# The first MLP product of a two-layer encoder by Strassen's scheme, on one core

## The chip, the cores and the metric

The kernel runs on one core of a Trainium2 chip. A core has five engines that run at the same time and wait for one another by semaphores: TensorE (PE; its weight loads are PEld), VectorE (DVE), ScalarE (ACT), GpSimd (POOL) and SyncE (SP, which here only issues DMAs). The metric is the device time of one execution in microseconds (us).

## The reference, cut to what matters

The model has two layers, each a mixer and an MLP, on 512 tokens of width 1024. The change is in the MLP alone:

```python
D_MODEL = 1024; SEQ = 512; D_FF = 4 * D_MODEL; DEPTH = 2
def _rmsnorm(x, g):
    y = x * lax.rsqrt(jnp.mean(x * x, axis=-1, keepdims=True) + RMS_EPS)
    return y * g
def _mlp(x, norm_g, w1, w2):
    h = _rmsnorm(x, norm_g)
    return jnp.square(jax.nn.relu(h @ w1)) @ w2
...
for layer in range(DEPTH):
    x = x + (_even_mixer if layer == 0 else _odd_mixer)(x, ...)
    x = x + _mlp(x, mlp_norm[layer], w_mlp_in[layer], w_mlp_out[layer])
```

All data are float32.

## The kernel before

The residual `xT` is held transposed: eight tiles of 128 features by 512 tokens. Every float32 product is made from three matmuls: each operand is split into a high part, rounded to the type `float32r` by a ScalarE cast, and a low part, the difference, by VectorE, and the product is high x high + high x low + low x high. The products of the activations with the norm's gain are split once per norm (`norm.xg`, a high and a low tile per feature block); the factor per token (`rb`, from `norm.rows()`) is applied where a result leaves PSUM.

Weights come from HBM in pieces of 512 KB. `load_w` issues the DMA on SyncE's queue into a raw buffer (`wraw`, three of them), and splits it into `whi` (line 158, ScalarE) and `wlo` (line 159, VectorE), two buffers each. The cast and the subtraction stand under `tc.high_priority(60)`: the framework lays the instructions of each engine in an order of its own, by readiness and a priority that follows the order of the source, and these two count as if they stood 60 instructions earlier.

`proj_a` makes 256 output features for all 512 tokens: over the 128-row blocks k of the contraction and two column tiles m, three matmuls with 128 x 128 weights and a moving operand 512 wide (lines 177 to 179), into two PSUM banks (tag `acc`, four banks; `aux` has the other four). With eight blocks that is 48 matmuls and two weight pieces, one for every four blocks. Then the two banks are handed to an evacuation function.

`mlp` runs four quarters q of the 4096 hidden features. In each, four calls of `proj_a` make 1024 hidden features from `w1`; the evacuation `ev` takes, per bank, a maximum with 0 and the factor (line 1030, VectorE), the square (1032, ScalarE), and the split into `hh` (1033, ScalarE) and `hl` (1034, VectorE). Four more calls of `proj_a` multiply the quarter's hidden features by `w2` and add to `xT` (line 1044, VectorE). In the last quarter of the last layer `store` does this with the tokens as output rows instead, through `proj_b` (lines 252 to 254), and writes the output.

In the even mixer, the last of the four attention pairs uses projections 256 wide (lines 201 to 203); these are the kernel's 256-wide float32r products of this kind.

Of the kernel before, what the change touches and what calls it, by code (L numbers as in the profile page):

```python
# [9 lines left out]
F32 = mybir.dt.float32  # L10
F32R = mybir.dt.float32r
AF = mybir.ActivationFunctionType
ALU = mybir.AluOpType
# [3 lines left out]
P = 128  # L17
S = 512
# [14 lines left out]
def hybrid_encoder_kernel(  # L33
# [18 lines left out]
    nc = tc.nc  # L52
    mm = nc.tensor.matmul
    act = nc.scalar.activation
    V = nc.vector
    G = nc.gpsimd

    consts = ctx.enter_context(tc.tile_pool(name="consts", bufs=1))
    resid = ctx.enter_context(tc.tile_pool(name="resid", bufs=1))
    wpool = ctx.enter_context(tc.tile_pool(name="wpool", bufs=2))  # L60
# [4 lines left out]
    def acc():  # L65
        return psum.tile([P, 512], F32, tag="acc", bufs=4, name="acc")

    def aux():
        return psum.tile([P, 512], F32, tag="aux", bufs=4, name="aux")
# [6 lines left out]
    gv = consts.tile([P, N_VEC], F32, name="gv")  # L76
# [15 lines left out]
    V.tensor_scalar(nsink, hb[:, 0:8], -1.0, None, op0=ALU.mult)  # L92
    rstd_c = consts.tile([P, 8], F32, name="rstd_c")

    consts.tile([P, 112], F32, name="filler")


    def after(ins, before):
# [63 lines left out]
    def proj_a(w, r0, nk, c0, xs, evac):  # L162

        ps = [acc(), acc()]
        chunks = {}

        def weights(kb):
            if kb not in chunks:
                rows = slice(r0 + kb * P, r0 + min(kb + 4, nk) * P)
                chunks[kb] = load_w([w[rows, c0 : c0 + 256]], 4)  # L170
            return chunks[kb]

        for k, m in [(k, m) for k in range(nk) for m in range(2)]:
            hi, lo = weights(k - k % 4)
            xh, xl = xs[k]
            cs = slice(m * P, (m + 1) * P)
            mm(ps[m], hi[:, k % 4, cs], xh, start=k == 0, stop=False)  # L177
            mm(ps[m], hi[:, k % 4, cs], xl, start=False, stop=False)  # L178
            mm(ps[m], lo[:, k % 4, cs], xh, start=False, stop=k == nk - 1)  # L179
        for m in range(2):  # L180
            evac(m, ps[m])
# [102 lines left out]
    xT = [resid.tile([P, S], F32, tag=f"xT{d}", name=f"xT{d}") for d in range(KT)]  # L284

    def new_xg():
        return [
            (
                resid.tile([P, S], F32R, tag=f"xh{d}", name=f"xh{d}"),
                resid.tile([P, S], F32R, tag=f"xl{d}", name=f"xl{d}"),  # L290
            )
            for d in range(KT)
        ]

    def split_gain(dst, src, gain):
        h, l = dst
        return (
            act(h, src, AF.Copy, scale=gain),
            V.scalar_tensor_tensor(l, src, gain, h.bitcast(F32), op0=ALU.mult, op1=ALU.subtract),  # L299
        )  # L300

    class Norm:


        def __init__(self, vec):
            self.vec = vec
            self.xg = new_xg()
            self.sum = stat.tile([P, S], F32, tag="sqsum", name="sqsum")
            self.n = 0

        def add(self, d):
            split_gain(self.xg[d], xT[d], gv[:, self.vec + d : self.vec + d + 1])
            if self.n == 0:
                act(self.sum, xT[d], AF.Square)
            else:
                sq = stat.tile([P, S], F32, tag="sq", bufs=2, name="sq")
                act(sq, xT[d], AF.Square)
                (G if self.vec == V_MLP else V).tensor_tensor(self.sum, self.sum, sq, op=ALU.add)
            self.n += 1
# [652 lines left out]
    def store(w, hid, pool):  # L972

        rows = {}

        def turn(kb):
            t = kb // 2
            for half in range(2):
                pt = aux()
                for j in range(4):  # L980
                    nc.tensor.transpose(
                        pt[:, j * P : (j + 1) * P],
                        xT[4 * half + j][:, t * P : (t + 1) * P],
                        ident,
                    )
                r = resid.tile([P, S], F32, tag=f"xh{2 * t + half}", name="rows")
                nc.scalar.copy(r, pt)
                rows[t, half] = r

        for half in range(2):  # L990

            def ev(t, ps):
                o = pool.tile([P, S], F32, tag="o", bufs=3, name="o")
                n = 256 if (t, half) == (NB - 1, 1) else 512
                for c in range(0, 512, n):
                    V.tensor_tensor(
                        o[:, c : c + n], ps[:, c : c + n], rows[t, half][:, c : c + n], op=ALU.add
                    )
                    (nc.scalar if c else nc.sync).dma_start(
                        out[t * P : (t + 1) * P, half * 512 + c : half * 512 + c + n],  # L1000
                        o[:, c : c + n],
                    )

            proj_b(
                [w[:, half * 512 : (half + 1) * 512]],
                512,
                hid,
                ev,
                post=None if half else turn,
            )  # L1010

    def mlp(layer, norm, on_final, last=False):
        with tc.tile_pool(name=f"mlp{layer}", bufs=1) as pool:
            rb = None
            for q in range(4):
                hid = [
                    (
                        pool.tile([P, S], F32R, tag=f"hh{k}", name="hh"),
                        pool.tile([P, S], F32R, tag=f"hl{k}", name="hl"),
                    )  # L1020
                    for k in range(8)
                ]
                for c in range(4):

                    def ev(m, ps):
                        nonlocal rb
                        rb = rb or norm.rows()
                        hh, hl = hid[2 * c + m]
                        t = pool.tile([P, S], F32, tag="t", bufs=2, name="t")
                        V.scalar_tensor_tensor(t, ps, 0.0, rb, op0=ALU.max, op1=ALU.mult)  # L1030
                        h = pool.tile([P, S], F32, tag="h", bufs=2, name="h")
                        act(h, t, AF.Square)
                        nc.scalar.copy(hh, h)
                        V.tensor_tensor(hl, h, hh.bitcast(F32), op=ALU.subtract)

                    proj_a(w1[layer], 0, 8, q * 1024 + c * 256, norm.xg, ev)
                if q == 3 and last:
                    store(w2[layer, 3072:4096], hid, pool)
                    continue
                for d0 in range(0, KT, 2):  # L1040

                    def ev2(m, ps):
                        d = d0 + m
                        V.tensor_tensor(xT[d], xT[d], ps, op=ALU.add)  # L1044
                        if q == 3:
                            on_final(d)

                    proj_a(w2[layer], q * 1024, 8, d0 * P, hid, ev2)
# [251 lines left out]

    even_mixer(n_mlp0)
    mlp(0, n_mlp0(), lambda d: n_odd().add(d))
    odd_mixer(n_odd(), n_mlp1)

    mlp(1, n_mlp1(), None, last=True)


# [75 lines left out]
```

## Time and profile before

| | before |
|---|---|
| median of 3 runs | 1361.17 us (1361.14 to 1361.97) |
| the profiled execution | 1362.33 us, of which its span is 1360.4 us |
| TensorE busy | 1340.6 us, 6210 matmuls |
| VectorE busy | 766.6 us |
| ScalarE busy | 591.2 us |
| GpSimd busy | 67.9 us |
| DMA | 124.64 MB, mean 92 GB/s |

A row of a group gives source line, engine, operation, tiles written <- read, shape, count, then busy us and mean ns of one, then the engine's idle us just before and what ended it. A row of a timeline gives start, duration, engine, line, and what was run, with the idle time before it in brackets. Neighbouring instructions of an engine overlap in their durations, so how long one takes its place in a stream is read from the starts.

### The profile page before, as it was taken

What the parts mean: (1) busy time and instruction counts of PE and PEld (TensorE: products, weight loads), DVE (VectorE), ACT (ScalarE), POOL (GpSimd) and SP (SyncE); (2) the same over time, 40 slices, a digit from 0 to 9 for tenths busy, and PEclk for the clock granted to TensorE, in tenths of its full rate; (3) what the DMA queues carried; (4) which work ended last, traced back from release to release, by engine and by line L of the source; (5) the groups of instructions that cost most, each with busy time, mean ns of one, the idle gap of its engine ahead of it and who ended that gap; (6) DMA issues with size and microseconds to landing.
All of it is one profiled execution on the core that took longest, in us unless ns stands there. A gap on an engine that the chain in (4) does not pass through costs nothing.

```text
span 1360.4 us, 16216 instructions
## 1 busy us (share of the span) xinstructions
PE 1340.6 (99%) x6210; PEld 1117.6 (82%) x6210; DVE 766.6 (56%) x1227; ACT 591.2 (43%) x1008; POOL 67.9 (5%) x80
## 2 busy tenths in 40 slices
PE   7999999999999999999999999999999999999998
PEld 6889887788888888888888888888888888888887
DVE  6788887633434434565758448547575344343433
ACT  4788775422313323344645445435354233142331
POOL 0223333000000000000000000000000000000000
PEclk9999999999999999999999999999999999999999
DMA  5322312333233223331221331321233333322322
GB/s 162 95 77 85 100 63 85 94 106 95 93 95 106 93 93 97 105 107 62 78 93 47 93 108 47 93 93 47 95 100 99 93 94 101 100 93 93 99 90 91
DMA packets 129502, 124.64 MB, mean 92 GB/s; under 512 B 9472, under 2 KB 122128, under 8 KB 129424
## 3 DMA queue, kind: packets, MB, share of 16 engines
q1 hardware_dynamic: 123648, 120.21, 28.4%
q10 hardware_dynamic: 5744, 3.37, 0.9%
q8 instruction: 49, 0.80, 0.2%
q14 instruction: 29, 0.24, 0.1%
q0 software_dynamic: 32, 0.01, 0.1%
HBM read 120.43 MB, written 3.15 MB: 91 GB/s over the span
## 4 chain that ended last, share of the span: by engine, by line
PE 90%; DVE 5%; ACT 2%; DMA 1%; issue 1%; SPq 0%; ACTq 0%; POOL 0%; DVEq 0%
PE acc L177 22%; PE acc L179 22%; PE acc L178 22%; PE acc L252 4%; PE acc L253 4%; PE acc L254 4%; PE aux L1204 1%; PE aux L1205 1%; PE aux L1206 1%; PE acc L201 1%; PE acc L203 1%; PE acc L202 1%; DVE wlo L159 1%; DMA qk<-in_x_dram 1%; PE aux L1191 1%
## 5 line engine op out<-in xcount | busy, mean ns | idle before, releaser
L158 ACT CAST whi<-wraw 128x1024 fp32r<-128x1024 f32 (+2 forms) x227 | 230.2, 1014 | 638.7 <-PE acc L178 530.5
L159 DVE TENSOR_TENSOR wlo<-wraw,whi 128x1024 fp32r<-128x1024 f32 (+2 forms) x218 | 261.0, 1197 | 290.6 <-ACT whi L158 289.4
L177 PE MATMUL acc<-xh,whi 128*128 128x512 f32 x784 | 305.2, 389 | 1.4 <-DVE xT L849 1.4
L178 PE MATMUL acc<-xl,whi 128*128 128x512 f32 x784 | 305.3, 389 | 0.3 <-DVE xl L299 0.3
L179 PE MATMUL acc<-xh,wlo 128*128 128x512 f32 x784 | 305.1, 389 | 0.0
L177 PE MATMUL acc<-hh,whi 128*128 128x512 f32 x448 | 174.3, 389 | 0.0
L178 PE MATMUL acc<-hl,whi 128*128 128x512 f32 x448 | 174.3, 389 | 0.0
L179 PE MATMUL acc<-hh,wlo 128*128 128x512 f32 x448 | 174.3, 389 | 0.0
L177 PEld LDWEIGHTS acc<-xh,whi 128*128 128x128 f32 x784 | 147.2, 188 | 32.5 <-DVE xT L849 1.8
L178 PEld LDWEIGHTS acc<-xl,whi 128*128 128x128 f32 x784 | 147.2, 188 | 31.3 <-DVE xl L299 1.0
L179 PEld LDWEIGHTS acc<-xh,wlo 128*128 128x128 f32 x784 | 147.2, 188 | 30.8 <-DVE wlo L159 0.2
L178 PEld LDWEIGHTS acc<-hl,whi 128*128 128x128 f32 x448 | 84.1, 188 | 17.5
L177 PEld LDWEIGHTS acc<-hh,whi 128*128 128x128 f32 x448 | 84.1, 188 | 17.4
L179 PEld LDWEIGHTS acc<-hh,wlo 128*128 128x128 f32 x448 | 84.1, 188 | 17.4
L1030 DVE SCALAR_TENSOR_TENSOR t<-acc,rstd_b 128x512 f32<-128x512 f32 x64 | 43.7, 691 | 77.1 <-PE acc L179 77.0
L1044 DVE TENSOR_TENSOR xT<-xT,acc 128x512 f32<-128x512 f32 x56 | 38.3, 687 | 74.8 <-PE acc L179 74.8
L252 PE MATMUL acc<-whi,xh 128*128 128x512 f32 x160 | 63.5, 397 | 0.0
L253 PE MATMUL acc<-wlo,xh 128*128 128x512 f32 x160 | 63.0, 394 | 0.0
L254 PE MATMUL acc<-whi,xl 128*128 128x512 f32 x160 | 62.8, 394 | 0.0
L201 PE MATMUL acc<-whi,xh 128*128 128x384 f32 (+1 forms) x160 | 52.6, 331 | 0.0
L202 PE MATMUL acc<-wlo,xh 128*128 128x384 f32 (+1 forms) x160 | 52.6, 329 | 0.0
L203 PE MATMUL acc<-whi,xl 128*128 128x384 f32 (+1 forms) x160 | 52.1, 326 | 0.0
(230 smaller groups left out, 1911.2 us busy)
## 6 DMA issues: line engine op xcount, KB each, us to landing
wraw<-in_w_mlp_in_dram SPq DMA_DIRECT2D x64, 512.0 KB
wraw<-in_w_mlp_out_dram SPq DMA_DIRECT2D x64, 512.0 KB
wraw<-in_w_in_o_dram SPq DMA_DIRECT2D x48, 512.0 KB
wraw<-in_w_out_o_dram SPq DMA_DIRECT2D x16, 512.0 KB
wraw<-in_w_in_e_dram SPq DMA_DIRECT2D x48, 128.0 KB
wraw<-in_w_in_e_dram SPq DMA_DIRECT2D x12, 256.0 KB
wraw<-in_w_out_e_dram SPq DMA_DIRECT2D x4, 512.0 KB
wraw<-in_w_out_e_dram SPq DMA_DIRECT2D x8, 256.0 KB
```

Of the source, the lines that this page charges most:

```text
L158: nc.scalar.copy(hu, used)
L159: eng.tensor_tensor(lu, used, hu.bitcast(F32), op=ALU.subtract)
L177: mm(ps[m], hi[:, k % 4, cs], xh, start=k == 0, stop=False)
L178: mm(ps[m], hi[:, k % 4, cs], xl, start=False, stop=False)
L179: mm(ps[m], lo[:, k % 4, cs], xh, start=False, stop=k == nk - 1)
L201: mm(o, lh, hi[:, k, :ncols], start=kb + k == 0, stop=False)
L202: mm(o, lh, lo[:, k, :ncols], start=False, stop=False)
L203: mm(o, ll, hi[:, k, :ncols], start=False, stop=kb + k == KT - 1)
L252: mm(o, lh, hi[:, k, :ncols], start=kb + k == 0, stop=False)
L253: mm(o, lh, lo[:, k, :ncols], start=False, stop=False)
L254: mm(o, ll, hi[:, k, :ncols], start=False, stop=kb + k == KT - 1)
L1030: V.scalar_tensor_tensor(t, ps, 0.0, rb, op0=ALU.max, op1=ALU.mult)
```

## The change

A unit is now 512 hidden features: two blocks of 256. Units 0 and 1 (the first quarter) keep `proj_a`. Units 2 to 7 of each layer are computed by seven products in place of eight, by Strassen's scheme in Winograd's form. The 1024 rows of the contraction are paired (even and odd 128-blocks), the 512 columns of the weights are halved, and so are the 512 tokens.

- `combine(i)`, called after each `proj_a` of units 0 and 1, makes once per layer the four sums of activations for one pair of feature blocks (two scaled ScalarE copies, four VectorE operations 256 wide, a cast and a subtraction 1024 wide).
- `load` brings the weights of a unit: A11, A12 and A22 by plain DMAs from SyncE into `sraw` (three buffers), the sums S1 and S3 by a plain DMA of A21 and a second DMA with accumulation, issued from GpSimd, into `ssum` (five buffers). S1 and S3 are asked for two units ahead, A11, A12 and A22 one.
- `total` makes S2 = S1 + A11 and S4 = S2 + A12 on VectorE. `high` and `low` split a block's four 128 x 256 weight tiles, for product j during product j - 2; products 0 and 1 of a unit are split in the unit before.
- `product` is 2 column tiles x 4 pairs x 3 matmuls with a moving operand 256 wide, into the two halves of one PSUM bank.
- `run` is the order of a unit: the seven products, four copies of a bank to SBUF (`keep`), three sums, four results. A result is evacuated 2 x 256 at a time. The last result of a unit is carried into the next one, or finished at once when the second product follows (`more` false).
- `run` stands in `tc.manual_schedule` for ScalarE and VectorE: within the region each of the two issues its instructions in the order of the source. The order on the other engines, and where instructions from outside the region fall among these, stay with the framework.
- `store` takes its output tiles from the tag `s` (five buffers) in place of `o` (three). A filler in the pool of constants is smaller.

The diff, cut to its core:

```diff
-    consts.tile([P, 112], F32, name="filler")
+    consts.tile([P, 80], F32, name="filler")
...
-                o = pool.tile([P, S], F32, tag="o", bufs=3, name="o")
+                o = pool.tile([P, S], F32, tag="s", bufs=5, name="o")
...
+        BLOCKS = ("A11", "A12", "S2", "S1", "S3", "S4", "A22")
+        INPUTS = ("B11", "B21", "U2", "U1", "T3", "B22", "T4")
...
+        def combine(self, i):
+            for m in range(2):
+                act(t, xT[d], AF.Copy, scale=gv[:, norm.vec + d : norm.vec + d + 1])
...
+            V.tensor_tensor(c[:, 0], b11, b12, op=ALU.subtract)
+            V.scalar_tensor_tensor(c[:, 1], c[:, 0], -1.0, b22, op0=ALU.mult, op1=ALU.subtract)
+            V.tensor_tensor(c[:, 2], b22, b12, op=ALU.subtract)
+            V.scalar_tensor_tensor(c[:, 3], c[:, 1], -1.0, b21, op0=ALU.mult, op1=ALU.subtract)
+            nc.scalar.copy(h, c)
+            V.tensor_tensor(l, c, h[:].bitcast(F32), op=ALU.subtract)
...
+                if name[0] == "S":
+                    nc.sync.dma_start(r[name], self.source(u, "A21"))
+                    second = self.source(u, "A22" if name == "S1" else "A11")
+                    G.dma_start(r[name], second, accum_op=ALU.add)
+                else:
+                    nc.sync.dma_start(r[name], self.source(u, name))
...
+        def product(self, u, j, ps, start):
+            for m in range(2):
+                o = ps[:, m * 256 : (m + 1) * 256]
+                for i in range(4):
+                    mm(o, h[:, i, cs], bh, start=first, stop=False, skip_group_check=True)
+                    mm(o, h[:, i, cs], bl, start=False, stop=False, skip_group_check=True)
+                    mm(o, l[:, i, cs], bh, start=False, stop=i == 3, skip_group_check=True)
...
+            a, b, c = acc(), aux(), acc()
+            self.product(u, 0, a, True)
+            load(u + 1, "A11")
+            ahead(2, False)          # high of product 2
+            lows()                   # low halves of results that are due
+            for step in last:        # the carried-over result (1, 0)
+                step()
+            ahead(2, True)           # low of product 2
+            self.product(u, 1, b, True)
+            s1 = keep(a); ahead(3, False); lows(); self.total(u, "S4"); ahead(3, True)
+            self.product(u, 2, a, False)
+            load(u + 1, "A12"); ahead(4, False); t = add(s1, b); result(0, 0, t, 1); ahead(4, True)
+            self.product(u, 3, c, True)
+            s2 = keep(a); ahead(5, False); lows(); ahead(5, True)
+            self.product(u, 4, a, False)
+            s5 = keep(c); load(u + 2, "S1"); load(u + 2, "S3"); ahead(6, False); ahead(6, True)
+            self.product(u, 5, c, False)
+            s3 = keep(a); load(u + 1, "A22"); ahead(7, False); t = add(s5, s3)
+            result(1, 1, t, -1); ahead(7, True); self.total(u + 1, "S2")
+            self.product(u, 6, a, False)
+            ahead(8, False); lows(); t = add(s2, c); result(0, 1, t, 1); ahead(8, True)
+            last.append(lambda: result(1, 0, a, -1))
+            if not more:
+                lows(); last.pop()(); lows()
...
-                    proj_a(w1[layer], 0, 8, q * 1024 + c * 256, norm.xg, ev)
+                for c in range(2):
+                    u = 2 * q + c
+                    if u < 2:
+                            proj_a(w1[layer], 0, 8, u * 512 + c2 * 256, norm.xg, ev)
+                            seven.combine(2 * u + c2)
...
+                    with tc.manual_schedule(
+                        engines={mybir.EngineType.DVE, mybir.EngineType.Activation}
+                    ):
+                        seven.run(u, evac, c == 0)
```

In the diff as shown, statements of `run` that stand on lines of their own are joined, and the comments are added.

More of the change, by code (lines that the diff above doesn't have):

```diff
@@ L1014, in mlp, with tmp, ev, evac @@
             rb = None
+            seven = Seven(pool, w1[layer], norm)
+            def tmp():
+                return pool.tile([P, S], F32, tag="s", bufs=5, name="s")
             for q in range(4):
[L1016 to L1021, printed above, removed]
-                ]
[L1023 to L1034, printed above, removed]
-                    proj_a(w1[layer], 0, 8, q * 1024 + c * 256, norm.xg, ev)
+                blocks = [
+                    [
+                        pool.tile([P, 2, S], F32R, tag=f"h{x}{k}", name=f"h{x}")
+                        for x in ("h", "l")
+                    ]
+                    for k in range(4)
+                ]
+                hid = [(h[:, m], l[:, m]) for h, l in blocks for m in range(2)]
+                for c in range(2):
+                    u = 2 * q + c
+                    if u < 2:
+                        for c2 in range(2):
+                            def ev(m, ps):
+                                nonlocal rb
+                                rb = rb or norm.rows()
+                                h, l = blocks[2 * c + c2]
+                                t = tmp()
+                                V.scalar_tensor_tensor(
+                                    t, ps, 0.0, rb, op0=ALU.max, op1=ALU.mult
+                                )
+                                act(t, t, AF.Square)
+                                nc.scalar.copy(h[:, m], t)
+                                V.tensor_tensor(
+                                    l[:, m], t, h[:, m].bitcast(F32), op=ALU.subtract
+                                )
+                            proj_a(w1[layer], 0, 8, u * 512 + c2 * 256, norm.xg, ev)
+                            seven.combine(2 * u + c2)
+                            if (u, c2) == (0, 1):
+                                seven.load(2, ("A11", "A12"))
+                            if (u, c2) == (1, 0):
+                                seven.load(2, ("S1", "S3"))
+                                for j in range(2):
+                                    seven.high(2, j)
+                                    seven.low(2, j)
+                        if u == 1:
+                            seven.load(2, ("A22",))
+                            seven.total(2, "S2")
+                            seven.load(3, ("S1", "S3"))
+                        continue
+                    def evac(fb, half, ps, sign, c=c):
+                        hs = slice(half * 256, (half + 1) * 256)
+                        h, l = (x[:, :, hs] for x in blocks[2 * c + fb])
+                        t = ps if sign > 0 or half else tmp()
+                        two = lambda v: v[:].rearrange("p (m t) -> p m t", m=2)
+                        V.scalar_tensor_tensor(
+                            two(t),
+                            two(ps),
+                            0.0,
+                            rb[:, hs].unsqueeze(1).to_broadcast([P, 2, 256]),
+                            op0=ALU.max if sign > 0 else ALU.min,
+                            op1=ALU.mult,
+                        )
+                        def high():
+                            act(t, t, AF.Square)
+                            nc.scalar.copy(h, two(t))
+                        def low():
+                            V.tensor_tensor(l, two(t), h.bitcast(F32), op=ALU.subtract)
+                        return high, low
+                    with tc.manual_schedule(
+                        engines={mybir.EngineType.DVE, mybir.EngineType.Activation}
+                    ):
+                        seven.run(u, evac, c == 0)
```

122 lines of the change are left out of this document (added).

## The prediction

> **What bounds the kernel now.** I read the page from the top: busy time, then the 40 slices of 34 us (each digit a tenth), and then the timelines.
>
> ```profile
> span 1360.4 us, 16216 instructions
> PE 1340.6 (99%) x6210; PEld 1117.6 (82%) x6210; DVE 766.6 (56%) x1227; ACT 591.2 (43%) x1008; POOL 67.9 (5%) x80
> ...
> PE   7999999999999999999999999999999999999998
> PEld 6889887788888888888888888888888888888887
> DVE  6788887633434434565758448547575344343433
> ACT  4788775422313323344645445435354233142331
> POOL 0223333000000000000000000000000000000000
> PEclk9999999999999999999999999999999999999999
> ```
>
> TensorE is busy in all but the first slice, at full granted clock; POOL is idle from slice 8 on. The MLPs (about 246 to 594 us and 1015 us to the end) have VectorE and ScalarE under half busy. So time here falls only with the time of the matmul stream, as long as nothing else becomes late. How long a matmul takes its place in the stream is read from starts, not durations: first the 256-wide ones that the even mixer has (36 rows in a row; first, last, and a weight load), then VectorE in one second-product stretch.
>
> ```profile
> 155.79 0.28 PE L202 MATMUL acc<-wlo,xh 128*128 128x256 f32 x1
> 159.98 0.28 PE L201 MATMUL acc<-whi,xh 128*128 128x256 f32 x1
> 159.98 0.19 PEld L202 LDWEIGHTS acc<-wlo,xh 128*128 128x128 f32 x1
> ...
> 354.86 1.37 DVE L1030 SCALAR_TENSOR_TENSOR t<-acc,rstd_b 128x512 f32<-128x512 f32 x2 [2.68 <-PE acc L179]
> 356.40 1.23 DVE L159 TENSOR_TENSOR wlo<-wraw,whi 128x1024 fp32r<-128x1024 f32 x1 [0.17 <-ACT whi L158]
> 357.96 1.29 DVE L1034 TENSOR_TENSOR hl<-h,hh 128x512 fp32r<-128x512 f32 x2 [0.33 <-ACT hh L1033]
> 361.84 1.22 DVE L159 TENSOR_TENSOR wlo<-wraw,whi 128x1024 fp32r<-128x1024 f32 x1 [2.59 <-ACT whi L158]
> 365.74 1.37 DVE L1030 SCALAR_TENSOR_TENSOR t<-acc,rstd_b 128x512 f32<-128x512 f32 x2 [2.68 <-PE acc L179]
> ```
>
> 256 wide: 4.19 us over 35 intervals, 0.1197 us each, every one with its own weight load. 512 wide: L1030 follows the end of each call of 48 matmuls, 354.86 to 365.74, 0.2267 us each. Two 256-wide ones cost 6% more than one 512-wide: that is the price of halving.
>
> **The matmuls.** A unit of 512 columns has 2x8x2x3 = 96 matmuls of 512: 21.76 us. By the scheme it has 7 products x 2 column tiles x 4 x 3 = 168 of 256: 20.11 us. Gain 1.65 us in each of 12 units (6 per layer): **-19.8 us**. Each product takes 24 x 0.1197 = 2.87 us.
>
> One page of the Trainium skill bears on this price: "TensorE: Matmul & The Clock Gate", section "Back-to-back issue gap", gives N/2.4 + 2.5 ns, so 109 ns at 256 and 216 at 512, by which the gain would be an estimated 2.4 us per unit, 29 in all. The starts above do not agree (119.7 and 226.7), and the measured ones decide.
>
> **ScalarE and VectorE inside a unit.** Prices by form:
>
> ```profile
> L159 DVE TENSOR_TENSOR wlo<-wraw,whi 128x1024 fp32r<-128x1024 f32 x197 | 242.1, 1229 | 287.5 <-ACT whi L158 287.2
> L158 ACT CAST whi<-wraw 128x1024 fp32r<-128x1024 f32 x199 | 209.5, 1053 | 629.5 <-PE acc L178 528.4 <-PE acc L254 64.6 <-issue 34.6
> L1030 DVE SCALAR_TENSOR_TENSOR t<-acc,rstd_b 128x512 f32<-128x512 f32 x64 | 43.7, 691 | 77.1 <-PE acc L179 77.0
> L1034 DVE TENSOR_TENSOR hl<-h,hh 128x512 fp32r<-128x512 f32 x64 | 41.4, 689 | 10.7 <-ACT hh L1033 10.7
> L1032 ACT ACTIVATE h<-t 128x512 f32<-128x512 f32 x64 | 36.6, 619 | 0.0
> L1033 ACT CAST hh<-h 128x512 fp32r<-128x512 f32 x64 | 36.0, 610 | 0.0
> L1208 ACT COPY of<-aux 128x512 f32<-128x512 f32 x16 | 9.1, 584 | 10.5 <-PE aux L1206 10.3
> L622 DVE TENSOR_TENSOR mixa_f<-aux,mixa_f 64x256 f32<-64x256 f32 x16 | 6.7, 418 | 0.3
> L298 ACT ACTIVATE xh<-xT,gv 128x512 fp32r<-128x512 f32 x24 | 17.1, 714 | 6.4 <-DVE xT L849 6.4
> ```
>
> Before, a unit has four weight splits and four evacuations: VectorE 4x1.23 + 4x(0.69+0.69) = 10.4 us, ScalarE 4x1.05 + 4x(0.62+0.61) = 9.1. After: VectorE 7 `low` and 2 `total` of 1.23, 4 evacuations and 4 low halves of 0.69, 3 sums of 0.69: 18.7 us of 20.1, 93%. ScalarE 7 `high` 1.05, 4 `keep` 0.58, 4 squares and casts 1.23: 14.6 us. So VectorE is nearly a second bound, and in source order. By product (0 to 6), VectorE has 2.6, 3.2, 2.6, 1.9, 1.2, 3.8, 3.3 us against 2.87. I laid the lists against each other with a handover of 0.04 us (`whi` to `wlo` in the rows above), neighbours overlapping by 0.06 (two of 0.69 take 1.29 to 1.37). Backlog starts in product 5 and reaches 2.0 us at the next unit's start. The first unit of a pair (c = 0) starts with empty lists and waits for nothing. In the second, ScalarE's `keep` of product 0 stands behind the cast of the carried-over result, and ends 0.34 us before product 2 may write that bank; the one before product 4 has 0.31 us, the weights of product 3 0.66. The lower end is therefore 0; with a handover of 0.15 and no overlap 1.75 us per second unit, 10.5 in all. I take 0.4, nearest to the measured handover, x 6 pairs: **+2.4** (0 to 10.5).
>
> **Where a pair ends.** The second product (`proj_a` on `w2`) needs its weight splits W0 at once and W1 after 24 matmuls, 5.4 us, hidden rows 4, 5 then, rows 6, 7 at 8.2 us. Its ScalarE and VectorE steps stand outside the ordered region and have the earlier priority (60), so W0 can go in during products 5 and 6; the covering work is these two products. After product 6 VectorE still has the rest of its backlog (2.0), W1, two low halves, one evacuation and the 1.2 us of ScalarE between them: rows 6, 7 are done 6.8 us after it if W1 goes into ScalarE's gap, 9.4 to 10.9 if W1 goes ahead of everything. Stall 0 to 2.6; I take 0.5, nearer the first because the gap is there, x 6: **+3** (0 to 16). Without that cover, see the first rival. `w2`'s own raw loads have three buffers that nothing else uses in these units.
>
> **The first two units of each layer** keep the old matmuls and get four `combine`: ScalarE 2x0.71 + 1.05, VectorE 4x0.42 + 1.23, so 10 and 12 us, and the first splits and sum of unit 2 (3.7).
>
> ```profile
> core 0: us, PE busy (x) PEld busy (x) DVE busy (x) ACT busy (x) POOL busy (x), PEclk, DMA share, GB/s
> 246.00:289.00 43.00, 42.81 (x189) 35.48 (x190) 23.62 (x30) 17.02 (x26) 0.00 (x0) 1.00 0.33 104
> ...
> 376.50:420.00 43.50, 43.50 (x194) 36.03 (x193) 15.27 (x16) 8.43 (x8) 0.00 (x0) 1.00 0.31 97
> ```
>
> VectorE comes to 39 of 43 us. The weight splits go first and have 5.4 us for 2.3 of work, so one foreign 1.23 us step ahead of them is covered; two are not quite. I take 1 per layer: **+2** (0 to 10). What is left over spills into the second product, where VectorE has 28 us free (second row).
>
> **DMAs.** A unit loads 7 pieces of 512 KB for 4. One piece now:
>
> ```profile
> 352.21 0.37 SPq L137 DMA_DIRECT2D wraw<-in_w_mlp_out_dram  x1
> ...
> 353.20:355.30 2.10, 2.10 (x11) 1.75 (x10) 0.44 (x1) 0.00 (x0) 0.00 (x0) 1.00 0.85 250
> ...
> hb<-in_heads_dram POOLq DMA_DIRECT2D x1, 12.0 KB, 6.7
> ```
>
> (The issue on SyncE's timeline; a row of the busy times by window, the DMA engines' share and GB/s last; the one issue from POOL, KB and us to landing.) It lands 3.1 us after issue and takes 1.8 us of the 16 engines; seven take 12.5 of 20.1 us, accumulation counted twice 16. SP issues five (1.9 us) in place of four. Plain pieces are asked for four products (11.5 us) or more ahead; they wait on SP for buffers read one or two products earlier, and what stands behind them (the next pieces, `w2`'s) has that lead too. The two accumulating ones go through POOL, wait there for their first piece, and have only each other behind them. The tight one is `S1`: asked for in product 4, needed in product 5 of the next unit, 8 products or 23 us, when both units belong to one pair (4 places; else a second product of 43.5 us lies between). No accumulating transfer is in the trace: as cheap as a plain one 3.1; dear, by the one POOL transfer (6.7 us for 128 rows) scaled to 512 rows, 26.8, so 29.9 with the first piece, 6.9 late. I take cheap, as a 512 KB piece is the nearest in kind: **0** (0 to +28). Five output buffers in place of three, and the smaller filler: 0 (the tail's wait for out DMAs is 1.4 us at most).
>
> **Sum.** -19.8 + 2.4 + 3 + 2 = -12.4 on the span of 1360.4, so 1348.0. That execution took 1362.33 in all; the three runs have 1361.17 at the median, 0.77 over the span: I predict 1348.8.
>
> **Rivals.**
> *The second product's first split comes late.* If W0 stands behind the ordered lists, ScalarE reaches it only after the last hidden cast, and the first matmul waits some 5.4 us (rest of the lists 3.1, split 2.3) at each of 6 pair ends: 32 in place of 3, 1378, slower. It decides once a pair end costs 2.6 us. For: ScalarE and VectorE are both fuller there. Against: the priority, and `whi` is free after product 4. 0.10.
> *VectorE overflows.* Operations 10 to 15% dearer than the rows give 1.1 to 1.7 us per second unit, 2.5 per pair end, 3 at the start: 8 + 15 + 3 - 19.8 = +6 at worst, about -1 midway: 1360, no change. For: 93% full, slack of 0.3 us. Against: the forms have the same prices everywhere in the trace. 0.15.
> *Accumulation is late:* 28 more, 1377. For: nothing shows its price. Against: the lead is seven times a plain piece. 0.06.
> *Loads do not overlap matmuls.* A load lasts 0.19 us; if each 256-wide matmul took that, a unit would take 31.9, 10 more than now: 1361 + 122 = 1483. Against: 35 intervals of 0.1197. 0.01. [...]
>
> **Chances.** The forecast's case 0.68, its own range 1341 (no stalls) to 1358. A run tells about 0.2% (2.7 us) from no change. Faster: 0.68 and a third of the overflow, 0.73; same: half of the overflow and a little of the late cases, 0.10; slower: late split, late sums, the rest of the overflow, 0.17. Range 1340 to 1368: the overflow whole, half-late splits.
>
> **What would show it.** Right: 7074 matmuls and loads (864 more); 256-wide starts 0.12 us apart; units 20.1 us from one first product 0 to the next; DVE near 890 us, ACT near 680; 143 MB moved. Wrong: idle TensorE before product 2 or 4 released by a ScalarE copy (lists), before the first `w2` matmul of a quarter released by `wlo` or `hl` (pair end), VectorE waiting for a DMA of `ssum` (accumulation), or 256-wide starts above 0.125 us.

## The result and the profile after

| | before | after |
|---|---|---|
| median of 4 runs each, same chip | 1361.16 us (1361.05 to 1361.97) | 1344.36 us (1343.98 to 1344.74) |
| the profiled execution | 1362.33 us, span 1360.4 us | 1344.74 us, span 1343.0 us |

The ratio is 0.9875 (95% interval 0.9858 to 0.9892): 16.8 us faster, where 12.4 were forecast. The page of the changed kernel, its busy times and the slices that answer to those of before:

```profile
span 1343.0 us, 18186 instructions
PE 1322.5 (98%) x7074; PEld 1142.8 (85%) x7074; DVE 874.8 (65%) x1363; ACT 676.3 (50%) x1116; POOL 99.6 (7%) x104
...
PE   8999999999999999999999999999999999999998
...
DVE  6788887864837647586748448547588567484553
ACT  4788776542624426444745445435366245262451
POOL 0222432110100000000000000000000000010000
PEclk9999999999999999999999999999999999999999
...
DMA packets 148519, 143.63 MB, mean 107 GB/s; under 512 B 10049, under 2 KB 141137, under 8 KB 148433
```

864 more matmuls take 18.1 us less busy time, and TensorE is as full as before from the second slice on. VectorE rose by 108 us and ScalarE by 85 without becoming the bound. Where the time went is read by stages, cut at the first matmul of each: a row gives the stretch, its length, then busy us and instructions of each engine, the granted clock, the DMA share and GB/s. The changed kernel's last three calls of the first quarter's first product (the first call runs ahead of the norm's factor), the second product behind them, a pair of units, the second product after it, and the last second product of the layer:

```profile
246.85:279.51 32.66, 32.66 (x145) 27.03 (x144) 26.00 (x39) 19.76 (x29) 2.44 (x2) 1.00 0.47 146
279.51:323.03 43.52, 43.52 (x193) 36.04 (x192) 21.49 (x26) 12.79 (x15) 2.74 (x3) 1.00 0.71 172
323.03:363.35 40.32, 40.32 (x338) 40.31 (x337) 29.98 (x34) 25.17 (x34) 5.13 (x4) 1.00 0.66 150
363.35:407.11 43.76, 43.76 (x195) 35.96 (x193) 20.62 (x24) 10.96 (x13) 0.00 (x0) 1.00 0.43 127
531.47:575.02 43.55, 43.55 (x194) 36.05 (x193) 24.55 (x31) 17.79 (x25) 0.00 (x0) 1.00 0.30 97
```

Of the kernel before, the same three calls, and the two stages that answer to a pair and the second product after it:

```profile
246.52:279.18 32.66, 32.66 (x145) 27.04 (x144) 18.85 (x24) 12.80 (x20) 0.00 (x0) 1.00 0.36 113
...
322.70:366.22 43.52, 43.52 (x193) 36.05 (x192) 19.16 (x23) 14.68 (x21) 0.00 (x0) 1.00 0.32 97
366.22:409.74 43.52, 43.52 (x193) 36.05 (x192) 16.57 (x19) 10.51 (x13) 0.00 (x0) 1.00 0.31 97
```

All six pairs take 40.31 or 40.32 us in place of 43.52: 3.20 x 6 = 19.2 us. The three calls of the first quarter take 32.66 in both kernels. The five second products that follow a pair lie between 43.55 and 43.76, 0.9 us in all over 43.52. The rest lies outside the MLPs' pairs: the first of those three calls in layer 0 starts 0.3 later, the odd mixer 0.6 shorter, and the stretch from the start of the last matmul to the end of the span 1.1 longer (4.98 for 3.89). 0.3 - 19.2 + 0.9 - 0.6 + 1.1 = -17.5, against the spans' difference of 17.4.

### The profile page after: what moved, and what is told of

Same layout as the page of the kernel before. It is cut to its first block, busy times and chain, and to the rows that moved or that the text cites. A ratio compares the mean times of both kernels' runs of the same rounds, so it can differ in the third digit from the quotient of the medians.

```text
span 1343.0 us, 18186 instructions
## 1 busy us (share of the span) xinstructions
PE 1322.5 (98%) x7074; PEld 1142.8 (85%) x7074; DVE 874.8 (65%) x1363; ACT 676.3 (50%) x1116; POOL 99.6 (7%) x104
## 2 busy tenths in 40 slices
DMA packets 148519, 143.63 MB, mean 107 GB/s; under 512 B 10049, under 2 KB 141137, under 8 KB 148433
## 4 chain that ended last, share of the span: by engine, by line
PE 90%; DVE 5%; ACT 2%; DMA 1%; issue 1%; POOL 0%; ACTq 0%; SPq 0%; DVEq 0%
PE acc L177 16%; PE acc L178 16%; PE acc L179 16%; PE acc L1116 5%; PE acc L1115 5%; PE acc L1114 5%; PE acc L252 4%; PE acc L253 4%; PE acc L254 4%; PE aux L1458 1%; PE aux L1459 1%; PE aux L1460 1%; PE acc L201 1%; PE acc L203 1%; PE acc L202 1%; PE aux L1116 1%
## 5 line engine op out<-in xcount | busy, mean ns | idle before, releaser
L159 DVE TENSOR_TENSOR wlo<-wraw,whi 128x1024 fp32r<-128x1024 f32 (+2 forms) x170 | 201.2, 1183 | 170.1 <-ACT whi L158 168.8
L177 PE MATMUL acc<-xh,whi 128*128 128x512 f32 x400 | 155.8, 389 | 0.7 <-DVE xT L849 0.7
L178 PE MATMUL acc<-xl,whi 128*128 128x512 f32 x400 | 155.9, 390 | 0.3 <-DVE xl L299 0.3
L179 PE MATMUL acc<-xh,wlo 128*128 128x512 f32 x400 | 155.8, 390 | 0.3 <-DVE wlo L159 0.3
L177 PEld LDWEIGHTS acc<-hh,whi 128*128 128x128 f32 x448 | 84.1, 188 | 17.4
L179 PEld LDWEIGHTS acc<-hh,wlo 128*128 128x128 f32 x448 | 84.1, 188 | 17.4
L177 PEld LDWEIGHTS acc<-xh,whi 128*128 128x128 f32 x400 | 75.1, 188 | 16.9 <-DVE xT L849 1.1
L178 PEld LDWEIGHTS acc<-xl,whi 128*128 128x128 f32 x400 | 75.1, 188 | 16.5 <-DVE xl L299 1.2
L179 PEld LDWEIGHTS acc<-xh,wlo 128*128 128x128 f32 x400 | 75.1, 188 | 16.4 <-DVE wlo L159 0.9
L1114 PE MATMUL acc<-uh,whi 128*128 128x256 f32 x288 | 81.5, 283 | 0.0
L1115 PE MATMUL acc<-ul,whi 128*128 128x256 f32 x288 | 81.5, 283 | 0.0
L1116 PE MATMUL acc<-uh,wlo 128*128 128x256 f32 x288 | 81.5, 283 | 0.0
```

The source lines that it names most:

```text
L159: eng.tensor_tensor(lu, used, hu.bitcast(F32), op=ALU.subtract)
L1114: mm(o, h[:, i, cs], bh, start=first, stop=False, skip_group_check=True)
L1115: mm(o, h[:, i, cs], bl, start=False, stop=False, skip_group_check=True)
L1116: mm(o, l[:, i, cs], bh, start=False, stop=i == 3, skip_group_check=True)
```

## The experiments

The kernel before ran 1361.7 to 1362.0 us (medians) on the same chips as the experiments. Each is an edit of the changed kernel, but for the one that is an edit of the kernel before.

**What the gain is made of: the halves without the scheme.** The kernel before, with the matmuls of units 2 to 7 cut into two of 256:

```diff
-                    proj_a(w1[layer], 0, 8, q * 1024 + c * 256, norm.xg, ev)
+                    proj_a(w1[layer], 0, 8, q * 1024 + c * 256, norm.xg, ev, q > 0)
```

> Edit: the kernel before, with each 512-wide matmul of units 2 to 7 of the first product cut into two of 256 tokens (192 per unit, same weights loaded twice, no seven products). Theory (a 256-wide matmul takes 0.120 us in any such stream, a 512-wide one 0.2267): a pair takes 46.1 in place of 43.5 us, 6 x 2.56 = 15.4 us more: 1376.6; then the omitted eighth product is worth 19.2 + 15.4 = 34.6 us and halving takes 15.4 of it. Rival (256-wide matmuls cost half of a 512-wide one, and the shortfall against 7/8 of the time lies elsewhere): 1361.2 within 1.

Measured 1377.71 us (1376.88 to 1379.44), ratio 1.0119 (1.0105 to 1.0133). Its pair, by window:

```profile
321.73:367.80 46.07, 46.07 (x386) 46.07 (x384) 19.24 (x23) 14.60 (x20) 0.00 (x0) 1.00 0.30 93
```

46.07 us over 384 matmuls is 0.1200 each. Halving alone costs 2.55 us per pair, 15.3 in all (16.0 by the medians), and leaving out the eighth product brings 46.07 - 40.32 = 5.75 per pair, 34.5 in all. The net gain is the small difference of the two: the stream's price of a 256-wide matmul, 6% above half a wide one, takes nearly half of what the scheme saves.

**The order by hand.** `tc.manual_schedule` removed; the framework orders ScalarE and VectorE there too:

```diff
-                    with tc.manual_schedule(
-                        engines={mybir.EngineType.DVE, mybir.EngineType.Activation}
-                    ):
-                        seven.run(u, evac, c == 0)
+                    seven.run(u, evac, c == 0)
```

> Edit: the ordered region around the unit is taken away, so the framework orders ScalarE and VectorE in the units too; the work is the same. Theory (the source order is what leaves every product its operands in time: a bank copy 0.6 us, the weights of product 3 1.0 us ahead in the second unit of a pair): another order puts some copy or split later than these margins, and the six pairs take more than 40.32 us each, 3 to 15 us in all: 1347 to 1359. Rival (the order is worth nothing, there is room for any): 1344.4 within 1 us, pairs 40.3 us.

Measured 1344.83 us (1343.99 to 1345.67), ratio 0.9874 (0.9858 to 0.9891): no difference. The windows of a pair and of the second product after it:

```profile
324.56:364.88 40.32, 40.32 (x338) 40.31 (x337) 31.80 (x37) 25.31 (x34) 5.13 (x4) 1.00 0.79 181
364.88:408.42 43.54, 43.54 (x194) 36.05 (x193) 18.29 (x21) 10.54 (x13) 0.00 (x0) 1.00 0.32 99
```

The pair is as long as before the edit and the second product has even lost its 0.22 us, so the rival held: the written order is worth nothing in time here. The framework's own order finds the slack too.

**The stall at a pair's end.** `low` of product 8 (the next unit's second split, which nothing needs soon) put after the last results (at the end of the branch `not more`) where the second product follows:

```diff
-            ahead(8, True)
+            if more:
+                ahead(8, True)
...
+                ahead(8, True)
```

> Edit: where a pair ends, the low part of the next unit's product 1 is made after the last results in place of before them (same instructions). Theory: the stall of the second product (0.1 to 0.2 us at hidden rows 6 and 7, five times, the last low half landing 8.4 us after product 6 where 8.2 are to be had) is VectorE's queue; 1.14 us less ahead of the results takes it away, the five second products take 43.52 in place of 43.74 us: 1 us less, 1343.4. Rival: the second product's own weight splits set it, and it stays at 43.74: 1344.4.

Measured 1344.16 us (1343.21 to 1345.96), ratio 0.9872 (0.9857 to 0.9886), and the second products stay at 43.72 and 43.74. VectorE's timeline, after the last matmul of the pair:

```profile
365.29 0.68 DVE L1271 SCALAR_TENSOR_TENSOR s<-s,rstd_b 128x512 f32<-128x512 f32 x1
367.32 0.69 DVE L1285 TENSOR_TENSOR hl<-s,hh 128x512 fp32r<-128x512 f32 x1 [1.35 <-ACT hh L1282]
367.93 0.68 DVE L1271 SCALAR_TENSOR_TENSOR s<-acc,rstd_b 128x512 f32<-128x512 f32 x1
369.34 1.23 DVE L159 TENSOR_TENSOR wlo<-wraw,whi 128x1024 fp32r<-128x1024 f32 x1 [0.72 <-ACT whi L158]
370.52 0.69 DVE L1285 TENSOR_TENSOR hl<-s,hh 128x512 fp32r<-128x512 f32 x1
```

The 1.22 us of `low` are gone from the way, but the last result (367.93) must still follow the low half of the result before it, in the order of the source, and VectorE stands idle for 1.35 us in front of that; then `w2`'s next split goes first. The step that was moved was not the one that the chain hung on. In a kernel below that also puts the last result ahead of those low halves (the third of those that do unit 1 by the scheme) the second products are 43.54 or 43.55, as they are in the free order: the stall of 0.2 us is this order's doing.

**How full VectorE is.** Two more subtractions of 128x1024 in every unit, writing the same low part again:

```diff
             ahead(3, True)
+            ahead(3, True)
+            ahead(3, True)
```

> Edit: the low part of product 3's weights is computed three times in place of once in each unit (the same values), 2.3 us more of VectorE's queue, 21 us of work for a unit of 20.16 us. Theory (VectorE in source order is almost a second bound, its lists leave 1.0 us before product 3 in the second unit of a pair and 3 us more in the first): the first unit stays free, the second waits 1.0 to 1.5 us before products 3 and 4: 6 to 9 us in all, 1350.5 to 1353.5. Rival (VectorE at 93% of a unit only looks full, its work lies beside the matmuls with room): under 1 us, 1344.4 to 1345.4.

Measured 1355.76 us (1355.34 to 1355.9), ratio 0.9955 (0.994 to 0.997): 11.4 us lost, where 6 to 9 were expected. A pair's window, and TensorE's waits in that window (us in all, times, longest):

```profile
323.72:366.09 42.37, 40.98 (x337) 40.46 (x336) 34.80 (x38) 24.86 (x34) 5.13 (x4) 1.00 0.64 144
```

```profile
PE acc L1116 <- DVE slo L1104: 1.2, 1, 1.2
PE acc L1114 <- ACT s L1128: 0.2, 1, 0.2
```

Each pair is 2.05 us longer. Where, the starts of the matmuls show; this is the second unit of the pair, at product 3:

```profile
352.78 0.28 PE L1115 MATMUL acc<-ul,shi 128*128 128x256 f32 x1
354.23 0.39 PE L1116 MATMUL acc<-uh,slo 128*128 128x256 f32 x1 [1.17 <-DVE slo L1104]
354.45 0.28 PE L1114 MATMUL acc<-uh,shi 128*128 128x256 f32 x1
```

The three subtractions write one tile, so the first matmul of product 3 that reads the low half (L1116) waits for the last of them. There the changed kernel has 1.25 us of slack (1.0 before the product starts, below, and two matmuls), and 2.5 us were added (3.74 for the three, 1.22 for one): 1.3 are missing. By starts the stream loses 1.33 us at this matmul and 0.10 at the next, 0.49 more before product 4, which waits for a ScalarE copy, and only 0.15 in the whole first unit, whose lists start empty: 2.07 in all. The waits above are shorter, 1.4 together, as a matmul counts there as busy for 0.28 us and takes its place in the stream for 0.12. So it is the slack at one deadline that decides, not VectorE's busy time, which is 34.8 of 42.4 us; the theory held in where the waits come (the second unit, before products 3 and 4), with 1.9 us there in place of 1.0 to 1.5. The waits have the names that the forecast's list stall would have had.

**The accumulating transfers.** First, with the second DMA of each sum left out; S1 and S3 are then A21 alone:

```diff
-                    G.dma_start(r[name], second, accum_op=ALU.add)
```

> Edit: the 24 accumulating transfers from GpSimd are left out, so S1 and S3 are A21 alone (the sums are not formed). Theory: the transfers cost nothing in the units (they land 7.9 us after issue, asked for 23 us ahead) and 1.1 us at the end of the kernel, where SyncE's and GpSimd's closing steps are longer than before: the time from the last matmul's start to the end falls from 4.98 to about 3.9 us, the pairs stay at 40.32, so about 1343.3. Rival A: the longer end has another cause: it stays at 5.0, 1344.4. Rival B: the transfers also slow something in the units or the first quarter: more than 1.5 us gained, seen in the pairs or between them.

Measured 1344.12 us (1343.13 to 1346.03), ratio 0.9871 (0.9857 to 0.9886), pairs 40.32: the transfers cost nothing that this can tell. Whether they lengthen the end stays open. From the start of the last matmul to the end of the span it took 4.98 us in the changed kernel's profiled run and 4.33 without the accumulation, but the other kernels with it had 4.1 to 4.96; without it, the kernel before had 3.89 and its halved form 4.02.

Then the sums asked for one unit later in the source:

```diff
-            load(u + 2, "S1")
-            load(u + 2, "S3")
+            if u > 2:
+                load(u + 1, "S1")
+                load(u + 1, "S3")
```

> Edit: S1 and S3 are asked for in product 4 of the unit before (units 4 to 7), where the kernel asks two units ahead: one product (2.9 us) before S2 needs S1, in place of eight. Theory (an accumulating transfer lands 7.9 us after issue, behind a plain piece of 3.1, so S1 needs 11 us, and VectorE in source order then holds everything behind S2): S2 comes about 6 us late in four units per layer, and a wait of 4 to 6 us follows in each (product 1 of the next unit, or the end of the pair): 32 to 48 us, 1376 to 1392. Rival A (it lands like a plain piece, 6.2 us for both): 1 to 2 us late, about 8 x 1: 1352. Rival B (the lead is worth nothing, there is room behind S2): 1344.4 within 1.

Measured 1344.87 us (1344.38 to 1345.32), ratio 0.9876 (0.9862 to 0.9889): no loss. GpSimd's timeline shows why (issue of the sum S1 of unit 4; VectorE's use of it, S2, starts at 362.23):

```profile
343.65 1.28 POOL L1076 DMA_DIRECT2D ssum<-in_w_mlp_in_dram  x1 [46.89 <-DMA ssum<-in_w_mlp_in_dram]
```

18.6 us of lead in place of 28.7 (issue at 333.61, use at 362.35 in the changed kernel). The later request took 10 us of lead, but the DMA still goes out 11 us before product 4 of unit 3 (354.6 us), behind which it stands in the source. It waits for its plain piece, issued at 337.91 behind a piece of `sraw` that had waited for a buffer; in the changed kernel the plain piece was issued at 328.93, when a split had set its own buffer free. So the position in the source is only part of what sets the lead: the buffers and SyncE's queue are the rest.

To make them late indeed, the sums of units 4 to 7 were asked for in the unit before, and their accumulations held behind a GpSimd operation on one column that reads the `keep` made during product 5:

```diff
+                        with tc.issue_after(gate):
+                            G.dma_start(r[name], second, accum_op=ALU.add)
...
+            if 2 < u < 7:
+                gate = pool.tile([P, 1], F32, tag="gate", bufs=2, name="gate")
+                g = G.tensor_tensor(gate, s3[:, 0:1], s3[:, 0:1], op=ALU.add)
+                self.load(u + 1, ("S1", "S3"), g.ins)
```

> Edit: the accumulating transfers of S1 and S3 of units 4 to 7 are held on GpSimd's queue behind a one-column GpSimd addition that reads the bank copy of product 5 in the unit before, so they start some 0.8 us into that product; S2 is due 4.8 us into it. (In e5_sums_late the transfers still started 18.6 us ahead of S2, since the framework issued them as soon as their buffer was free.) Theory (an accumulating transfer takes 7.9 us to land, and what stands behind S2 in VectorE's order waits with it): S2 about 4 us late; about 3 us lost before product 1 of the next unit inside a pair, 4 us at the end of a pair, 2 + 2 such places per layer: 28 us, 1372. Rival A (it lands like a plain piece, 3.1 us): S2 is in time, 1344.4. Rival B (S2 late, but with room behind it): under 5 us, below 1350.

Measured 1411.37 us (1407.52 to 1415.69), ratio 1.0366 (1.0345 to 1.0387): 67 us over the changed kernel, far more than expected. Waits of TensorE and of VectorE over the whole run, then windows around three of them, and the first of these cut where the clock changes:

```profile
PE acc L177 <- ACT hh L1286: 31.7, 4, 8.7
PE aux L1120 <- DVE slo L1108: 17.7, 4, 5.2
...
DVE ssum L1089 <- DMA ssum<-in_w_mlp_in_dram: 59.0, 9, 9.7
```

```profile
368.00:382.00 14.00, 5.28 (x15) 3.56 (x14) 8.41 (x10) 3.44 (x5) 0.00 (x0) 0.67 0.78 184
436.00:450.00 14.00, 8.82 (x63) 8.61 (x62) 7.04 (x10) 5.07 (x8) 1.02 (x1) 0.80 0.92 197
466.00:482.00 16.00, 8.54 (x32) 6.41 (x31) 7.98 (x10) 4.64 (x7) 0.00 (x0) 0.78 0.93 200
...
368.80:372.70 3.90, 0.16 (x1) 0.00 (x0) 0.54 (x1) 0.00 (x0) 0.00 (x0) 1.00 0.90 142
372.70:377.69 4.99, 0.00 (x1) 0.01 (x1) 4.78 (x7) 1.30 (x3) 0.00 (x0) 0.50 0.60 143
377.69:382.94 5.25, 5.25 (x12) 3.84 (x13) 3.09 (x4) 2.14 (x3) 0.00 (x0) 0.50 0.81 270
```

VectorE waits for the sum, all that stands behind S2 in its order waits with it, and TensorE waits 49.4 us for results and splits. This is the rival "accumulation late" of the prediction, made true: it has the mechanism that was described, and it was only not met. The expected size was wrong twice. The held accumulations took longer to land than 7.9 us (the row of the tile `ssum` over 340 to 480 us):

```profile
DMA to landing us min/median/max: 8.3/11.5/14.1
```

All six there were issued in twos. That alone does not explain it, as the two of 536.32 us landed after 7.0 and 9.3; the cause stays open. And the waits explain 49 of the 70.9 us by which the profiled execution's span (1413.9) is longer than the changed kernel's: the granted clock falls to 0.67 to 0.80 in the windows around them. Cut finer, it stays 1.00 for the first 3.7 us of this wait, is 0.50 for the rest of it, and 0.50 still for 5.25 us of work behind it, of which half is lost: 2.6 us. Behind a wait inside a pair it is 0.50 for 4.09 us of work (447.12 to 451.21), 2.0 lost. With four waits of each kind that is an estimated 19 us, most of the 21.5 that are left. The Trainium skill, "TensorE: Matmul & The Clock Gate", section "Why this matters for your kernels", says that a gap of more than some 3 us between bursts of matmuls puts the clock back to one half; the waits of 4 to 9 us here agree in that the clock falls, and the 1.2 us waits of the kernel with two more subtractions (1.00 in its window) in that it does not. One stretch does not agree: in the third kernel of the next part the clock falls as well, just behind waits of only 1.6 and 0.3 us:

```profile
237.05:240.46 3.41, 3.41 (x9) 2.63 (x9) 3.41 (x4) 2.98 (x5) 3.25 (x3) 0.50 0.76 259
```

**Can unit 1 be done by the scheme too?** By the pairs it would save another 1.6 us per layer. It was tried in four ways. In the first, unit 0 alone keeps the old matmuls, `combine` runs for all four pairs of blocks during it with the subtraction on GpSimd, and `low` of product 8 stands last:

```diff
-                    if u < 2:
+                    if u < 1:
...
-            V.tensor_tensor(l, c, h[:].bitcast(F32), op=ALU.subtract)
+            G.tensor_tensor(l, c, h[:].bitcast(F32), op=ALU.subtract)
...
+                            seven.combine(2 * c2)
+                            seven.combine(2 * c2 + 1)
+                        seven.load(1, ("S1", "S3"))
```

> Edit: unit 1 of each layer by seven products too, all four combines after unit 0's calls, their subtraction of 1024 elements on GpSimd, and the low part of product 8 last at a pair's end. Theory (a unit is worth 1.6 us, and VectorE decides whether it is kept): VectorE has about 27 us of work in the 27.5 us before unit 1's product 2, so between 3.2 us less (1341) and a wait of 2 us in each layer that eats it (1345). Rival (the first quarter has room like the others): 1341.0.

Measured 1387.21 us (1386.84 to 1389.97), ratio 1.0194 (1.018 to 1.0208), slower than the kernel before. The waits around the first quarter, and three windows there:

```profile
PE acc L1114 <- ACT s L1128: 20.8, 1, 20.8
POOL ul L1048 <- ACT uh L1047: 18.1, 3, 13.0
...
ACT whi L1099 <- DVE ssum L1085: 13.8, 1, 13.8
DVE ssum L1085 <- DMA ssum<-in_w_mlp_in_dram: 13.6, 1, 13.6
```

```profile
263.80:284.60 20.80, 0.18 (x2) 0.00 (x0) 6.01 (x12) 5.57 (x8) 10.46 (x7) 0.59 0.64 119
284.60:290.00 5.40, 5.22 (x29) 4.95 (x30) 5.33 (x6) 2.73 (x5) 0.00 (x0) 0.67 1.18 244
290.00:296.00 6.00, 6.00 (x52) 6.00 (x51) 3.49 (x4) 4.22 (x6) 1.01 (x1) 1.00 0.76 254
```

TensorE waits 20.8 us for a `keep` of unit 1. ScalarE, which would make it, stands in source order behind splits whose sum S2 waits for S1's accumulation, and this was issued from GpSimd only behind the subtractions of `combine`, at 272.74 us. These hold the buffers of `ssum` too: SyncE's plain pieces of the sums waited 21.9 us for them. Then 5.4 us at a mean clock of 0.67 (0.50 up to 288.18 us, 1.00 after) cost 1.8 more. Without the hand-made order:

> Edit: as v1_unit1_too, with the order of ScalarE and VectorE in the units left to the framework. Theory: the pair ends lose their 0.2 us as in e1_free_order (1 us in all) and the combines may mix with unit 1's splits by readiness: 1340 to 1343. Rival: the free order puts combines behind splits and unit 1 waits for its sums of activations: above 1345.

1383.36 us (1383.2 to 1384.86), ratio 1.0161 (1.0147 to 1.0175), a wait of 18.4 us per layer. ScalarE now makes the `keep` in time and waits 8.9 us for the transfer itself: the order is not the cause, the late transfer is. So the next version asks for all of unit 1's weights ahead of unit 0, and takes the buffers of `combine` from `wraw`, to leave `ssum` to the sums; the last result of a pair goes ahead of the low halves:

```diff
+                        seven.load(1, ("S1", "A11", "S3", "A12", "A22"))
...
-            c = pool.tile([P, 4, 256], F32, tag="ssum", bufs=5, name="c")
+            c = wpool.tile([P, 1024], F32, tag="wraw", bufs=3, name="c")[:].rearrange(
+                "p (j c) -> p j c", j=4
+            )
```

> Edit: unit 1 of each layer by seven products too; its weights are asked for before unit 0, all four combines after unit 0's two calls (their sums in a raw weight buffer), everything of them on VectorE as in the changed kernel; at a pair's end the last result goes ahead of the low halves and of the low part of product 8. Theory (v1_unit1_too lost its 40 us to S1, whose transfer stood on GpSimd's queue behind the combines' subtractions; without that VectorE is what remains, with about 29 us of work for 27.5): 1.6 us less per layer and a wait of 1 to 3 us: 1341 to 1347. Rival (the transfer was not the cause): above 1370.

1390.46 us (1388.88 to 1393.18), ratio 1.0214 (1.02 to 1.0228). The sums are in time now, and unit 0's own second call waits:

```profile
PE acc L177 <- ACT whi L158: 10.3, 1, 10.3
```

Its raw weights need the buffers that `combine` holds: SyncE's queue waited 20.3 us in that stretch for VectorE's last step of `combine`. The pairs behind are 40.32 and the second products 43.54, as good as any. With the order left to the framework and the subtraction on GpSimd it is worse:

> Edit: as v3_unit1_early, with the combines' subtraction on GpSimd and the order of ScalarE and VectorE in the units left to the framework. Theory: VectorE has 4.6 us less before unit 1's product 2 (24.7 of 27.5 us) and the pair ends wait for nothing: 1340 to 1342, below the changed kernel by 2 to 4 us. Rival (GpSimd's 2.4 us steps make the sums of activations late): above 1344.

1411.7 us (1411.52 to 1413.0), ratio 1.0371 (1.0357 to 1.0385), with waits of TensorE for `whi` (25.1 us in three) and for GpSimd's `ul` (7.5 in four); the two changes were not made apart. In all four the trouble is a late piece (a sum behind GpSimd's queue, raw weights without a buffer, or in the last a slow subtraction too) in a stretch of one unit; that no arrangement of buffers would do it was not shown. No version beats the changed kernel by more than a measurement can tell.

## Why the prediction was right, by its steps

- **The matmuls: -19.8 forecast, -19.2 measured.** The sum by starts was right to 3%: 40.32 us for 336 matmuls is 0.1200, against 0.1197 in the even mixer. The rival that loads don't overlap is excluded by the same starts. By the formula of the Trainium skill, "TensorE: Matmul & The Clock Gate", section "Back-to-back issue gap", which is given there for an isolated matmul and not for a stream, the gain would have been an estimated 29; this does not agree.
- **The lists of ScalarE and VectorE: +2.4 forecast, 0 measured.** The order and the slack were as laid out, only roomier. From the timeline of the second unit of a pair, the `keep` before product 2 and the matmuls around it:

```profile
347.73 0.58 ACT L1128 COPY s<-acc 128x512 f32<-128x512 f32 x1
...
348.83 0.28 PE L1116 MATMUL aux<-xh,slo 128*128 128x256 f32 x1
...
348.95 0.28 PE L1114 MATMUL acc<-uh,whi 128*128 128x256 f32 x1
```

  The copy ends at 348.31 and product 2 starts at 348.95: 0.64 us of slack where the lists had given 0.34. The second copy has 0.77 (forecast 0.31), product 3's weights 1.0 (0.66). Neighbours on VectorE overlap by 0.085 us, not 0.06, and a handover takes 0.03: laid again with these, the lists give an estimated 0.67, 0.79 and 1.03, which fits, but both numbers come from the trace that they are to explain. The stall of 0.4 us per pair was an allowance on top of a calculation that had come out positive; the mis-sized term is that allowance. The rival of dearer operations did not come: a split costs 1.22 us and the 512-wide steps 0.68 to 0.69, as the rows before had it. VectorE's 93% was a sum of durations: in a pair's window it is busy 29.98 of 40.32 us, 74%, as only 31 of its 40 operations lie there (with three of the second products), and overlaps count once.
- **The pair's end: +3 forecast, +0.9 measured.** The stall was met in four of the five, at hidden rows 6 and 7 as described; the mis-sized term is 0.5 us, which measured 0.2. On ScalarE's and VectorE's timelines `w2`'s splits go in where they were put, and the last hidden rows come just late:

```profile
368.79 1.05 ACT L158 CAST whi<-wraw 128x1024 fp32r<-128x1024 f32 x1 [0.96 <-PE acc L178]
369.75 0.62 ACT L1279 ACTIVATE s<-s 128x512 f32<-128x512 f32 x1
370.40 0.62 ACT L1280 CAST hh<-s 128x512 fp32r<-128x512 f32 x1
369.88 1.23 DVE L159 TENSOR_TENSOR wlo<-wraw,whi 128x1024 fp32r<-128x1024 f32 x1 [0.72 <-ACT whi L158]
371.05 0.69 DVE L1283 TENSOR_TENSOR hl<-s,hh 128x512 fp32r<-128x512 f32 x1
371.80 0.50 PE L178 MATMUL acc<-hl,whi 128*128 128x512 f32 x1
```

  The last `hl` ends at 371.74, 8.4 us after the pair's last matmul gave way to `w2` at 363.35, where 8.2 is in time: between the forecast's 6.8 and 9.4. What it had not seen is that `w2`'s third split (368.79 and 369.88) gets in ahead of the last result's halves. At the last pair of a layer no unit follows, and the second product takes 43.55: the splits of the next unit's first two products and its S2, three steps of 1.22 us on VectorE, are missing there. The later one of the two `low` alone would not do it, as the edit that moved it showed. The rival "first split late" did not come: `w2`'s first matmul starts at 363.35, 0.12 us after the last one of product 6 (363.23).
- **The first two units: +2 forecast, 0 measured.** VectorE is busy 26.0 of 32.66 us in the last three calls and 21.5 of 43.52 in the second product behind them, and the two stages are as long as before to 0.01 us. Over the 43 us that the forecast took (246.33 to 289.33 here, the three calls and 10 us of the second product) it is busy 34.5 us, not 39. The 1 us per layer was an allowance too.
- **The DMAs: 0 forecast, 0 measured**, with 143.63 MB as forecast. An accumulating piece lands 7.9 us after issue at the median (6.2 to 11.8), between the ends taken, 3.1 and 26.8, and nearer the first. So the price that the forecast took (3.1) was too low by 4.8 us, and its 0 held by the room in the lead: 7.9 behind a plain piece of 3.1 is 11.0, against 23. The lead was called 23 us by the position in the source; for the sum S1 of unit 4 it is 28.7, and 18.6 where it was asked for a unit later. That the price would have mattered had the lead been gone, the held sums show.
- **The end (the output buffers): 0 forecast.** 1.1 us were seen in one run, and not settled.

The forecast's span stood 5.0 us over the measured one: 6.5 for three allowances that didn't come (2.4, 2.1 and 2), less 0.6 of the matmuls' gain and 0.8 from start, odd mixer and end; its time stood 4.4 over the median. For the lists and the first units the allowance stood on the losing side of a calculation that said "fits"; for the pair's end it lay inside the calculation's range.

## What to carry to other kernels

Halving a matmul's width to save one product in eight pays only the difference between two larger numbers (here 34.5 saved, 15.3 paid), so the price per start at the new width is the first thing to read, from a stretch of the same kernel that already runs it. A helper engine that looks nearly full by a sum of durations is free as long as each copy that frees a bank and each split is in time: lay its lists with the measured overlap, believe them, and test the margin by adding work. A transfer's lead is given by when its buffer comes free and what its queue waits for, and only in part by where it stands in the source.

## What the runs showed of the hardware that was not expected

- An accumulating transfer of 512 KB takes 7.9 us from issue to landing (6.2 to 11.8), 11.5 (8.3 to 14.1) for six that were held and issued in twos; one plain piece of the kernel before took 3.1.
- A wait of TensorE costs more than its length. In a wait of 8.7 us the granted clock was 1.00 for the first 3.7 us, then 0.50, and 0.50 still for 5.25 us of work behind it; in the longest wait, 20.8 us, it was again 1.00 for 3.7 us, then 0.50 until 3.4 us behind its end. Waits of up to 1.2 us left it at 1.00 in the kernel with two more subtractions, but waits of 1.6 and 0.3 us close together stood ahead of 3.41 us at 0.50.
- The price of a 256-wide matmul, 0.1200 us, is the same with VectorE busy 74% of the stage as with 42% (the kernel before in halves, 19.24 of 46.07 us).
